# GLA gate function moved behind a PSUM copy, and softmax scaling moved to ScalarE, in a two-layer hybrid decoder kernel

## The chip, the cores and the metric

The kernel runs on one core of a Trainium2 chip, in one launch. The metric is the device time of that launch in microseconds (us). Below, PE is the matrix engine (PEld its weight loads), DVE the vector engine, ACT the scalar engine, POOL GpSimd, SP the engine that issues most DMAs. PSUM is the memory that PE writes, SBUF the working memory. All engines run their own instructions in a fixed order and wait for one another by semaphores.

## The reference

Two layers, 1024 tokens, width 1024, float32. A layer has a mixer and a channel part; the mixer runs gated linear attention (GLA, 4 heads) beside latent softmax attention (MLA, 4 heads) and projects both back. Cut to what the change touches:

```
# GLA: chunked linear attention with a data-dependent decay; then
o = gla_chunked(q, k, v, log_a)
o = rms_norm(o, gla_out_norm) * silu(g_o)            # g_o = columns of h @ w_in: the "gate"
# MLA: causal softmax attention, 128 queries at a time
s = (q_nope k_nope^T + q_pe k_pe^T) * scale
p = softmax(where(mask, s, -inf))
out = p v
mixed = concat([gla_out, mla_out]) ; x += gate_a * (mixed @ w_out)
# channel part
x += gate_f * (relu(h W1)^2 W2)
```

## The kernel before, in words

Every large product is made of three matmuls on rounded halves (`mm3`, lines 161 to 163: high times high, high times low, low times high). Weights arrive by DMA and are split into a high and a low part by ACT (line 314) and DVE (line 315). The channel part uses seven products instead of eight for a two by two block product; its lines are 1287 to 1290 (operands combined and split) and 1415 (results added).

The mixer works on two halves of the tokens, A and B, of 512 each. Its steps stand in a table of short words, `PROGRAM`: `L` latents, `T` what follows them, `Q` GLA queries and keys, `W` GLA scores, `v` and `g` GLA values and gates, `O` GLA outputs, `u`/`U` a head's queries and keys, `a` softmax attention of one head and two query blocks, and so on. `gA OA` stand next to each other, and so do `gB` and, after a few steps, `OB`.

GLA scores (`gla_scores`) walk through seven levels of a block hierarchy. A level has a decay update on DVE (lines 973, 978), exponentials on ACT (972, 974), products on POOL (944, 975), copies into block form on ACT (948), small matmuls into PSUM bank `g` (929) and masked writes from that bank on DVE (955, 983, 990). The bank has two buffers.

Gates (`gates`, lines 1029 to 1042) are four token blocks of 128 x 512 products in four PSUM banks. For each, ACT computes |x| from PSUM (1036), then exp and log (1037, 1038), DVE reads PSUM again for min(x,0) minus that (1039), ACT takes exp (1040), and DVE multiplies the PSUM product by it into SBUF (1041). The bank is free when 1041 is done.

In softmax attention (`softmax_pair`) DVE takes the row maximum (721), ACT the exponentials with their sum (736), DVE the reciprocal of the sum (740) and the scaling of the row block by it (741), before PE transposes the block (756), ACT and DVE split the transposed block (759, 760), and PE multiplies it with the values (lines 161 to 163 again).

The order on each engine is not the order of the code: a scheduler lists the instructions by what it takes to be ready, with the program's order as the priority. A change in one place moves instructions in many others.

Of the kernel before, what the change touches and what calls it, by code (L numbers as in the profile page):

```python
# [15 lines left out]
AF = mybir.ActivationFunctionType  # L16
ALU = mybir.AluOpType
# [109 lines left out]
def hybrid_kernel(  # L127
# [7 lines left out]
    V, S, G, PE = nc.vector, nc.scalar, nc.gpsimd, nc.tensor  # L135
# [16 lines left out]
    def bank_of(tags):  # L152
        i = turn.get(tags, 0)
        turn[tags] = i + 1
        return bank(tags[i % len(tags)])

    def tmp():
        return tp.tile([P, 512], F32, tag="t", name="tmp")

    def mm3(o, lh, ll, rh, rl, start, stop):  # L160
        PE.matmul(o, lh, rh, start=start, stop=False)  # L161
        PE.matmul(o, lh, rl, start=False, stop=False)  # L162
        PE.matmul(o, ll, rh, start=False, stop=stop)  # L163
# [251 lines left out]
    def bc(a, n):  # L415
        return a.unsqueeze(len(a.shape)).broadcast_to(list(a.shape) + [n])
# [195 lines left out]
    def inproj_tok(l, hf, kind, w, hs, tg):  # L612

        pss = [bank_of(tg) for _ in range(4)]
        for q in range(4):
            u = U[l, hf, kind, q]
            get(u)
            for t in range(4):
                for k2 in range(2):
                    h = hs[q * 2 + k2]  # L620
                    wh, wl = uw(u, k2, 0, w)
                    mm3(pss[t][:, 0:w], R(h[:, t * P:(t + 1) * P]), R(h[:, 512 + t * P:512 + (t + 1) * P]), wh, wl,
                        q == 0 and k2 == 0, q == 3 and k2 == 1)
            drop(u)
        return pss

    def layer_mixer(l, hA, make_hB):
# [70 lines left out]
        def softmax_pair(gp, Qn, Kn, Qr, ts_):  # L698
            Pt, pk = [], []
            for t in (2 * gp, 2 * gp + 1):  # L700
                n = (t + 1) * P
                hq, tq = t // 4, (t % 4) * P
                qh = R(Qn[hq][:, tq:tq + P])
                ql = R(Qn[hq][:, 512 + tq:512 + tq + P])
                qr = R(Qr[hq][:, tq:tq + P])
                nch = (n + 511) // 512
                nm = sp.tile([P, 2], F32, tag="nm", name="nm")
                sm = sp.tile([P, 2], F32, tag="sm", name="sm")
                pss = []
                for cc in range(nch):  # L710
                    w = min(512, n - cc * 512)
                    ps = bank_of(ts_)
                    o = ps[:, 0:w]
                    kh, kl = R(Kn[cc][:, 0:w]), R(Kn[cc][:, 512:512 + w])
                    mm3(o, qh, ql, kh, kl, True, False)
                    last = cc == nch - 1
                    PE.matmul(o, qr, R(kpe[cc][:, 0:w]), start=False, stop=False)
                    PE.matmul(o, qr, R(kpe[cc][:, 512:512 + w]), start=False, stop=not last)
                    if last:
                        PE.matmul(o[:, w - P:w], ident_bf, causal_bf, start=False, stop=True)  # L720
                    V.tensor_reduce(nm[:, cc:cc + 1], o, AX.X, ALU.max, negate=True)
                    pss.append((o, w))
                if nch == 2:
                    V.tensor_tensor(nm[:, 0:1], nm[:, 0:1], nm[:, 1:2], op=ALU.min)
                if gp == 1:
                    p_ = AR.alloc()
                    pk.append(p_)
                    p_ = p_[:, 0:n]
                elif gp == 0:
                    if t == 0: pk.append(AR.alloc())  # L730
                    p_ = pk[0][:, t * P:t * P + n]
                else:
                    p_ = AR.alloc()
                    pk.append(p_)
                for cc, (o, w) in enumerate(pss):
                    S.activation(p_[:, cc * 512:cc * 512 + w], o, AF.Exp, bias=nm[:, 0:1], accum_out=sm[:, cc:cc + 1])
                if nch == 2:
                    V.tensor_tensor(sm[:, 0:1], sm[:, 0:1], sm[:, 1:2], op=ALU.add)
                rc = sp.tile([P, 1], F32, tag="rc", name="rc")
                V.reciprocal(rc, sm[:, 0:1])  # L740
                V.tensor_scalar(p_[:, 0:n], p_[:, 0:n], rc, None, op0=ALU.mult)
                Pt.append(p_)
            return Pt, pk

# [74 lines left out]
        def used(hf):  # L819
            left[hf] -= 1  # L820
            if left[hf] == 0:
                AR.free(*hsb[hf])
# [206 lines left out]
        def gates(hf):  # L1029
            x = hv[hf]  # L1030
            x.g = [AR.alloc(), AR.alloc()]
            x.g3 = [a.rearrange("p (t n) -> p t n", t=2) for a in x.g]
            pss = inproj_tok(l, hf, "g", 512, hsb[hf], tags[5])
            for t in range(4):
                e = tmp()
                S.activation(e, pss[t], AF.Abs)
                S.activation(e, e, AF.Exp, scale=-1.0)
                S.activation(e, e, AF.Ln, bias=1.0)
                V.scalar_tensor_tensor(e, pss[t], 0.0, e, op0=ALU.min, op1=ALU.subtract)
                S.activation(e, e, AF.Exp)  # L1040
                V.tensor_tensor(x.g3[t // 2][:, t % 2, :], pss[t], e, op=ALU.mult)
            used(hf)

        def gla_out(hf):
            x = hv[hf]
            q, kdT, v3, g3, AT, eb = x.q, x.kdT, x.v3, x.g3, x.AT, x.eb
            ssq = sp.tile([P, 16], F32, tag="ssqg", name="ssqg")
            rst = sp.tile([P, 16], F32, tag="rstg", name="rstg")
            for tt in range(4):
                j, t = tt // 2, tt % 2  # L1050
                o = bank_of(tags[6])
                first = True
                if hf * 4 + tt > 0:
                    for p in range(2):
                        PE.matmul(o[:, p * 256:(p + 1) * 256], q[:, p * 512 + tt * P:p * 512 + (tt + 1) * P], state[:, p, :],
                                  start=first, stop=False, skip_group_check=True)
                        first = False
                for h in range(4):
                    PE.matmul(o[:, h * P:(h + 1) * P], AT[j][:, t * 512 + h * P:t * 512 + (h + 1) * P],
                              v3[j][:, t, h * P:(h + 1) * P], start=first, stop=(h == 3), skip_group_check=True)  # L1060
                    first = False
                if hf * 4 + tt < 7:
                    kvp = bank_of(tags[6])
                    for p in range(2):
                        PE.matmul(kvp[:, p * 256:(p + 1) * 256], kdT[:, (tt * 2 + p) * P:(tt * 2 + p + 1) * P],
                                  v3[j][:, t, p * 256:(p + 1) * 256], start=True, stop=True)
                    for p in range(2):
                        for e in range(2):
                            rs, cs_ = slice(e * 64, e * 64 + 64), slice(e * P, e * P + P)
                            st = state[rs, p, cs_]  # L1070
                            V.scalar_tensor_tensor(st, st, eb[rs, p * 4 + tt:p * 4 + tt + 1],
                                                   kvp[rs, p * 256 + e * P:p * 256 + (e + 1) * P], op0=ALU.mult, op1=ALU.add)
                sq = tmp()
                S.activation(sq, o, AF.Square)
                V.tensor_reduce(ssq[:, tt * 4:tt * 4 + 4], sq.rearrange("p (a n) -> p a n", a=4), AX.X, ALU.add)
                rstd_small(rst[:, tt * 4:tt * 4 + 4], ssq[:, tt * 4:tt * 4 + 4], ((0, 4, 128),), 4)
                gt = g3[j][:, t, :]
                g4 = gt.rearrange("p (a n) -> p a n", a=4)
                G.tensor_tensor(g4, g4, bc(rst[:, tt * 4:tt * 4 + 4], P), op=ALU.mult)
                V.tensor_tensor(gt, o, gt, op=ALU.mult)  # L1080
            x.mt = [AR.alloc(), AR.alloc()]
            for h in range(4):
                ps = bank_of(tags[6])
                for t in range(4):
                    PE.transpose(ps[:, t * P:(t + 1) * P], g3[t // 2][:, t % 2, h * P:(h + 1) * P], ident)
                S.activation(x.mt[h // 2][:, (h % 2) * 512:(h % 2) * 512 + 512], ps, AF.Identity, scale=gcol("go", l))
            AR.free(q, kdT, *x.v, *x.g, *AT)
# [368 lines left out]
```

## Time and profile before

| | |
|---|---|
| time, median of 3 runs | 2327.41 us (2325.14 to 2329.38) |
| profiled execution | 2325.83 us, span 2324.0 us |
| PE busy | 2226.7 us (96%) |
| DVE busy | 1777.6 us (76%) |
| ACT busy | 1135.3 us (49%) |
| POOL busy | 255.4 us (11%) |

The span is one execution as the hardware profiler saw it. A busy share is an average over very different stages, so the stage in which an engine waits matters more than its total. In the views below, "idle before" is the time for which an engine did nothing before an instruction, and the name behind the arrow is what ended that wait. Counts in a stretch that ends inside a step can split a pattern: 32 scalings per layer are 29 in the stretch that is used here.

### The profile page before, as it was taken

What the parts mean: (1) busy time and instruction counts of PE and PEld (TensorE: products, weight loads), DVE (VectorE), ACT (ScalarE), POOL (GpSimd) and SP (SyncE); (2) the same over time, 40 slices, a digit from 0 to 9 for tenths busy, and PEclk for the clock granted to TensorE, in tenths of its full rate; (3) what the DMA queues carried; (4) which work ended last, traced back from release to release, by engine and by line L of the source; (5) the groups of instructions that cost most, each with busy time, mean ns of one, the idle gap of its engine ahead of it and who ended that gap; (6) DMA issues with size and microseconds to landing.
All of it is one profiled execution on the core that took longest, in us unless ns stands there. A gap on an engine that the chain in (4) does not pass through costs nothing.

```text
span 2324.0 us, 29252 instructions
## 1 busy us (share of the span) xinstructions
PE 2226.7 (96%) x11016; PEld 1854.6 (80%) x11016; DVE 1777.6 (76%) x2519; ACT 1135.3 (49%) x1759; POOL 255.4 (11%) x236
## 2 busy tenths in 40 slices
PE   6979899999999998998999999999999999999998
PEld 3868788888788886887778888888888888877887
DVE  4887769757888888989894755997665867887794
ACT  3565646534732384433454545665365228633341
POOL 0042323100030000000011332320002000000000
PEclk8989999999999999999999999999999999999999
DMA  9632200136668655765784431004354654365462
GB/s 350 198 98 87 84 24 7 47 126 209 199 201 278 219 177 175 251 209 201 250 295 174 142 132 51 10 1 132 132 160 139 196 185 145 124 224 196 163 208 82
DMA packets 238450, 365.01 MB, mean 157 GB/s; under 512 B 11846, under 2 KB 146148, under 8 KB 238308
## 3 DMA queue, kind: packets, MB, share of 16 engines
q1 hardware_dynamic: 237760, 362.66, 47.5%
q8 instruction: 87, 1.43, 0.3%
q14 instruction: 55, 0.45, 0.1%
q10 hardware_dynamic: 548, 0.48, 0.1%
HBM read 325.73 MB, written 37.36 MB: 156 GB/s over the span
## 4 chain that ended last, share of the span: by engine, by line
PE 71%; DVE 11%; DMA 9%; issue 4%; ACT 2%; POOL 1%; SPq 0%; DVEq 0%; POOLq 0%; ACTq 0%
PE ps_m L162 9%; PE ps_m L163 9%; PE ps_m L161 9%; PE ps_s L162 7%; PE ps_s L163 7%; PE ps_s L161 7%; PE ps_g L163 4%; PE ps_g L162 4%; PE ps_g L161 4%; DMA s<-in_w_ada_dram 3%; DMA s<-in_w_mlp_down_dram 2%; PE ps_x L163 2%; PE ps_x L162 2%; PE ps_x L161 2%; DMA s<-in_w_mlp_up_dram 1%
## 5 line engine op out<-in xcount | busy, mean ns | idle before, releaser
L314 ACT CAST s<-s 128x1024 fp32r<-128x1024 f32 (+2 forms) x298 | 307.2, 1036 | 476.8 <-DVE s L311 259.2
L162 PE MATMUL ps_m<-s,s 128*128 128x512 f32 (+2 forms) x1212 | 460.9, 381 | 15.8 <-DVE s L1290 14.0
L161 PE MATMUL ps_m<-s,s 128*128 128x512 f32 (+2 forms) x1212 | 460.0, 383 | 10.6 <-ACT s L1289 4.7
L163 PE MATMUL ps_m<-s,s 128*128 128x512 f32 (+2 forms) x1212 | 457.0, 378 | 1.6 <-DVE s L315 1.6
L315 DVE TENSOR_TENSOR s<-s,s 128x1024 fp32r<-128x1024 f32 (+2 forms) x282 | 337.2, 1204 | 125.8 <-ACT s L314 105.5
L161 PE MATMUL ps_s<-s,s 128*128 128x512 f32 (+5 forms) x928 | 357.8, 389 | 5.0 <-ACT s L448 4.0
L163 PE MATMUL ps_s<-s,s 128*128 128x512 f32 (+5 forms) x928 | 355.5, 384 | 1.3 <-DVE s L315 1.3
L162 PE MATMUL ps_s<-s,s 128*128 128x512 f32 (+5 forms) x928 | 355.9, 384 | 0.0
L311 DVE TENSOR_TENSOR s<-s,s 128x1024 f32<-128x1024 f32 x160 | 198.9, 1245 | 117.2 <-DMA s<-in_w_mlp_up_dram 73.6
L162 PEld LDWEIGHTS ps_m<-s,s 128*128 128x128 f32 x1212 | 229.4, 189 | 60.9 <-DVE s L1290 17.4
L161 PEld LDWEIGHTS ps_m<-s,s 128*128 128x128 f32 x1212 | 229.1, 189 | 55.6 <-ACT s L1289 5.9
L163 PEld LDWEIGHTS ps_m<-s,s 128*128 128x128 f32 x1212 | 228.7, 189 | 41.9 <-DVE s L315 2.4
L1289 ACT CAST s<-s 128x1024 fp32r<-128x1024 f32 x140 | 146.8, 1051 | 185.5 <-DVE s L1287 53.3
L161 PEld LDWEIGHTS ps_s<-s,s 128*128 128x128 f32 x928 | 175.6, 189 | 40.6 <-ACT s L448 4.2
L163 PEld LDWEIGHTS ps_s<-s,s 128*128 128x128 f32 x928 | 175.8, 189 | 35.6 <-issue 1.9
L162 PEld LDWEIGHTS ps_s<-s,s 128*128 128x128 f32 x928 | 176.2, 190 | 32.0 <-issue 0.6
L162 PE MATMUL ps_g<-s,s 128*128 128x512 f32 (+1 forms) x506 | 195.2, 387 | 0.4 <-DVE s L1290 0.4
L161 PE MATMUL ps_g<-s,s 128*128 128x512 f32 (+1 forms) x506 | 194.6, 388 | 0.1
L163 PE MATMUL ps_g<-s,s 128*128 128x512 f32 (+1 forms) x506 | 194.4, 387 | 0.1
L1290 DVE TENSOR_TENSOR s<-s,s 128x1024 fp32r<-128x1024 f32 x140 | 171.2, 1227 | 13.3 <-ACT s L1289 9.7
L162 PE MATMUL ps_x<-s,s 128*128 128x512 f32 (+3 forms) x362 | 124.2, 345 | 1.9 <-DVE s L760 1.9
L161 PE MATMUL ps_x<-s,s 128*128 128x512 f32 (+3 forms) x362 | 122.4, 343 | 2.4 <-DVE s L760 2.4
(322 smaller groups left out, 3491.2 us busy)
## 6 DMA issues: line engine op xcount, KB each, us to landing
s<-in_w_mlp_up_dram SPq DMA_DIRECT2D x192, 512.0 KB
s<-in_w_mlp_down_dram SPq DMA_DIRECT2D x192, 512.0 KB
s<-in_w_ada_dram SPq DMA_DIRECT2D x80, 512.0 KB
s<-in_w_in_dram SPq DMA_DIRECT2D x36, 512.0 KB
s<-in_w_ada_dram SPq DMA_DIRECT2D x32, 256.0 KB
xd<-s SPq DMA_DIRECT2D x16, 512.0 KB
s<-in_w_out_dram SPq DMA_DIRECT2D x16, 512.0 KB
s<-xd SPq DMA_DIRECT2D x16, 512.0 KB
```

The lines of the kernel that those rows point to most:

```text
L161: PE.matmul(o, lh, rh, start=start, stop=False)
L162: PE.matmul(o, lh, rl, start=False, stop=False)
L163: PE.matmul(o, ll, rh, start=False, stop=stop)
L311: V.tensor_tensor(raw[:, :n], raw[:, :n], u.second[:, :n], op=ALU.add if u.sign > 0 else ALU.subtract)
L314: (V.tensor_copy if u.eng[-2] == "v" else S.copy)(R(u.hi[:, :n]), raw[:, :n])
L315: (V if u.eng[-1] == "v" else G).tensor_tensor(R(u.lo[:, :n]), raw[:, :n], u.hi[:, :n], op=ALU.subtract)
L1289: S.copy(R(hi), t)
L1290: V.tensor_tensor(R(lo), t, hi, op=ALU.subtract)
```

## The change

In `gates` each of the four PSUM products is now copied to SBUF by ACT and nothing else is done there. The gate function, unchanged in its arithmetic, stands at the head of `gla_out` and reads and overwrites the SBUF copy. In `softmax_pair` the scaling of the probabilities by the reciprocal of their sum is an ACT instruction with a per-partition scale instead of a DVE instruction. The lines behind the first change keep their text and shift by up to two; the gate function's lines 1036 to 1041 become 1045 to 1050, and the copy is line 1035.

```
-                V.tensor_scalar(p_[:, 0:n], p_[:, 0:n], rc, None, op0=ALU.mult)
+                S.activation(p_[:, 0:n], p_[:, 0:n], AF.Copy, scale=rc)
...
             for t in range(4):
-                e = tmp()
-                S.activation(e, pss[t], AF.Abs)
-                S.activation(e, e, AF.Exp, scale=-1.0)
-                S.activation(e, e, AF.Ln, bias=1.0)
-                V.scalar_tensor_tensor(e, pss[t], 0.0, e, op0=ALU.min, op1=ALU.subtract)
-                S.activation(e, e, AF.Exp)
-                V.tensor_tensor(x.g3[t // 2][:, t % 2, :], pss[t], e, op=ALU.mult)
+                S.copy(x.g3[t // 2][:, t % 2, :], pss[t])
...
         def gla_out(hf):
...
+            for tt in range(4):
+                gt, e = g3[tt // 2][:, tt % 2, :], tmp()
+                S.activation(e, gt, AF.Abs)
+                S.activation(e, e, AF.Exp, scale=-1.0)
+                S.activation(e, e, AF.Ln, bias=1.0)
+                V.scalar_tensor_tensor(e, gt, 0.0, e, op0=ALU.min, op1=ALU.subtract)
+                S.activation(e, e, AF.Exp)
+                V.tensor_tensor(gt, gt, e, op=ALU.mult)
             for tt in range(4):
```

DVE in the first layer's scores of half A, before; `s_165` and `s_166` hold the gates, `ps_m` and `ps_s` are their PSUM banks, `s_154` and `s_155` the scores:

```order
L990 COPY_PREDICATED s_154_1162<-lvm,ps_g 128x256x2
L973 TENSOR_TENSOR s_160_1171<-s_119_882 128x512
L1039 SCALAR_TENSOR_TENSOR tmp<-ps_m,tmp 128x512
L990 COPY_PREDICATED s_155_1163<-lvm,ps_g 128x256x2
L1039 SCALAR_TENSOR_TENSOR tmp<-ps_s,tmp 128x512
L1041 TENSOR_TENSOR s_165_1347<-ps_s,tmp 128x512
L978 TENSOR_TENSOR s_119_882<-s_119_882 128x32x16
L990 COPY_PREDICATED s_154_1162<-lvm,ps_g 128x128x4
```

And now, the stretch of the same engine in which the gate function's instructions stand:

```order
L990 COPY_PREDICATED s_154_1162<-lvm,ps_g 128x64x8
L1048 SCALAR_TENSOR_TENSOR tmp<-s_165_1347,tmp 128x512
L973 TENSOR_TENSOR s_161_1172<-s_119_882 128x512
L990 COPY_PREDICATED s_155_1163<-lvm,ps_g 128x64x8
L1048 SCALAR_TENSOR_TENSOR tmp<-s_165_1347,tmp 128x512
L1048 SCALAR_TENSOR_TENSOR tmp<-s_166_1348,tmp 128x512 x2
L978 TENSOR_TENSOR s_119_882<-s_119_882 128x16x32
L1050 TENSOR_TENSOR s_165_1347<-s_165_1347,tmp 128x512 x2
L990 COPY_PREDICATED s_154_1162<-lvm,ps_g 128x32x16
```

The eight DVE instructions of the gate function stay among the masked writes of the scores; they stand two levels later, and both their inputs are SBUF tiles.

ACT at the same place, now (before, the same instructions stand one by one between the others, each |x| read from a PSUM bank):

```order
L1035 COPY s_166_1348<-ps_m 128x512
L1035 COPY s_166_1348<-ps_s 128x512
L974 ACTIVATE s_160_1171<-s_160_1171 128x512
L1035 COPY s_165_1347<-ps_m 128x512
L1035 COPY s_165_1347<-ps_s 128x512
L972 ACTIVATE s_161_1172<-s_119_882 128x512
L1045 ACTIVATE tmp<-s_165_1347 128x512 x2
L1045 ACTIVATE tmp<-s_166_1348 128x512 x2
L314 CAST s_193_1741<-s_192_1739 128x1024
L948 COPY s_159_1167<-s_160_1171 64x8x64 x2
L974 ACTIVATE s_161_1172<-s_161_1172 128x512
L1046 ACTIVATE tmp<-tmp 128x512 x4
```

The gate function's ACT work comes in runs of four, ahead of copies (948) and exponentials (974) of the scores.

DVE in the first layer's attention, before, around the scaling of a block of 640 keys (`s_313` is the block):

```order
L738 TENSOR_TENSOR sm<-sm 128x1
L740 RECIPROCAL rc<-sm 128x1
L741 TENSOR_SCALAR s_313_3189<-s_313_3189,rc 128x640
L662 TENSOR_TENSOR s_308_3100<-ps_m,s_308_3100 128x256
L1075 TENSOR_REDUCE ssqg<-tmp 128x4
```

And ACT now, around the scaling of the same block:

```order
L736 ACTIVATE s_313_3197,sm<-ps_s,nm 128x512
L736 ACTIVATE s_313_3197,sm<-ps_s,nm 128x128
L646 COPY s_306_3078<-ps_m 128x384
L741 ACTIVATE s_313_3197<-s_313_3197,rc 128x640
L667 ACTIVATE s_309_3130<-s_306_3078 128x768
L1076 ACTIVATE tmp<-ps_g 128x512
L660 COPY s_307_3107<-ps_m 128x256
```

The scaling has left DVE's order and stands in ACT's, one copy behind the exponentials whose sum it needs, with a square (667) and PSUM copies (1076, 660) queued behind it.

## Rows read from the trace of the kernel before

**Rows 1.** Page, part 1: busy time of the engines, share of the span, instructions.
```profile
PE 2226.7 (96%) x11016; PEld 1854.6 (80%) x11016; DVE 1777.6 (76%) x2519; ACT 1135.3 (49%) x1759; POOL 255.4 (11%) x236
```
**Rows 2.** Windows: length, PE, PEld, DVE, ACT, POOL busy, PE clock, DMA share, GB/s.
```profile
143.00:183.00 40.00, 26.15 (x145) 24.01 (x145) 38.97 (x49) 29.05 (x48) 17.01 (x12) 0.79 0.18 51
260.00:290.00 30.00, 23.10 (x172) 20.82 (x171) 27.38 (x34) 25.34 (x45) 14.16 (x9) 1.00 0.26 74
320.00:475.00 155.00, 143.57 (x980) 127.64 (x978) 132.69 (x329) 93.85 (x244) 36.38 (x46) 0.97 0.12 36
...
1405.00:1430.00 25.00, 23.23 (x149) 21.19 (x148) 20.23 (x33) 17.66 (x35) 5.82 (x5) 0.93 0.17 56
1455.00:1580.00 125.00, 114.05 (x807) 101.48 (x806) 112.58 (x283) 82.67 (x216) 36.33 (x46) 0.99 0.05 14
```
**Rows 3.** PE's waits from 143 to 183 us, the longest: total, times, longest one.
```profile
PE ps_g L929 <- DVE s L990: 6.5, 6, 1.9
```
**Rows 4.** PE's waits from 260 to 290 us.
```profile
PE ps_g L929 <- DVE s L990: 2.9, 3, 1.2
PE ps_g L929 <- ACT s L948: 2.7, 2, 1.6
...
PE ps_s L161 <- DVE s L1041: 0.4, 1, 0.4
```
**Rows 5.** PE's waits from 320 to 475 us, the longest.
```profile
PE ps_x L756 <- DVE s L741: 1.9, 2, 1.3
PE ps_x L161 <- DVE s L760: 1.5, 2, 0.9
PE ps_g L756 <- DVE s L468: 1.5, 1, 1.5
PE ps_g L1065 <- DVE s L1080: 1.0, 1, 1.0
PE ps_m L161 <- ACT s L1093: 0.9, 1, 0.9
PE ps_x L162 <- DVE s L760: 0.9, 1, 0.9
PE ps_g L692 <- POOL s L607: 0.8, 1, 0.8
```
**Rows 6.** Timeline, DVE and PE near 356 us: start, length, what.
```profile
355.89 0.15 DVE L740 RECIPROCAL rc<-sm 128x1 f32<-128x1 f32 x1
...
356.69 1.15 DVE L741 TENSOR_SCALAR s<-s,rc 128x768 f32<-128x768 f32 x1
...
357.90 1.25 PE L756 MATMUL ps_x<-cs,s 128*128 128x128 f32 x6 [1.35 <-DVE s L741]
```
**Rows 7.** Line 741 on DVE from 320 to 475 us: count, busy us, mean ns.
```profile
L741 DVE TENSOR_SCALAR s<-s,rc 128x128 f32<-128x128 f32 (+7 forms) x29 | 14.9, 517 | 0.6
```
**Rows 8.** ACT instructions, run (L463, L1026) and 320 to 475 us: count, busy, mean.
```profile
L463 ACT ACTIVATE s<-tmp,mod 128x512 f32<-128x512 f32 x32 | 22.4, 730 | 13.1 <-DVE tmp L462 13.1
L1093 ACT CAST s<-s 128x512 fp32r<-128x512 f32 x8 | 5.0, 630 | 2.2 <-PE ps_m L163 2.1
L314 ACT CAST s<-s 128x1024 fp32r<-128x1024 f32 x3 | 3.1, 1049 | 4.8 <-DMA s<-in_w_out_dram 4.8
L1026 ACT COPY s<-ps_s 128x512 f32<-128x512 f32 x8 | 4.7, 587 | 13.8 <-PE ps_s L163 13.8
```
**Rows 9.** Lines 1039, 978, 424 on DVE: minimum, median, maximum ns, when.
```profile
L1039 DVE SCALAR_TENSOR_TENSOR tmp<-ps_m,tmp x8: 669/679/690, 146.3 to 1413.2; 128x512 f32<-128x512 f32 x8
L978 DVE TENSOR_TENSOR s<-s x28: 671/692/1814, 139.2 to 1404.4; 128x512 f32<-128x512 f32 x28
L424 DVE TENSOR_TENSOR s<-s,tmp x42: 676/685/693, 479.5 to 1695.6; 128x512 f32<-128x512 f32 x42
```
**Rows 10.** Timelines of DVE and POOL near 165 us.
```profile
164.69 1.56 POOL L944 TENSOR_TENSOR s<-s,s 128x512 f32<-128x512 f32 x1 [0.68 <-ACT s L972]
...
165.05 1.75 DVE L978 TENSOR_TENSOR s<-s 128x512 f32<-128x512 f32 x1
```

## The prediction

> **What bounds the kernel now.** I read the page's first part first: PE is busy for 2226.7 of 2324.0 us [rows 1]. DVE's 76% and ACT's 49% are averages, so neither is a bound by itself; what can be won lies in the 97 us in which PE does nothing, and the next question is where they are and who ends them. The windows answer the first half. The two stretches of GLA scores in the first layer leave PE idle for 13.9 us of 40 and 6.9 of 30, and there DVE is busy for 38.97 and 27.38 us: DVE is the bound. The two attention stretches leave it idle for 11.4 us of 155 and 10.9 of 125, with DVE at 86% and 90%. In the second layer the scores cost little, 1.8 of 25 us, because other matrix work stands between them [rows 2]. The waits give the second half: in the scores PE waits for the masked writes of line 990 (6.5 and 2.9 us), and in the second of them as long for ACT's copies, 2.7 us [rows 3, 4]; in attention nearly every wait is for DVE, the longest for the scaling that the change moves, 1.9 us [rows 5]. So both edits touch the engine that PE waits for.
>
> **The scaling goes to ACT.** It removes 29 instructions and 14.9 us from DVE in the first attention stretch [rows 7]. Their lengths grow with the keys, and ACT's I take from the nearest rows: 0.73 us for 512 columns with a per-partition operand, and (1049 - 630) / 512 = 0.82 ns for each further column [rows 8]. For 128 to 1024 columns that is 0.42 to 1.15 us, 6.3 us for one head's eight blocks, 0.79 on average, 22 to 23 us for the 29. Without the operand's 0.1 us it would be 19 to 20. DVE falls from 132.7 to 117.8 of 155 us, ACT rises from 93.9 to about 116.
>
> *What that frees.* One wait shows it: the reciprocal began at 355.89 and took 0.15, the scaling began only at 356.69 behind other DVE work and took 1.15, and PE lost 1.35 us [rows 6]. ACT's 0.94 us, begun behind the reciprocal, would end 0.8 us sooner. Of the 11.4 us idle, 0.9 are for ACT and twice 0.8 for POOL, so some 8 are for DVE [rows 5]. What waits behind a filled engine waits about as busy is to free: 86 to 14 before, 76 to 24 after, so by 46% less. That is 3.7 us a layer, 7.4 in both (the second stretch has the same pattern of waits and 10.9 us idle). The granted clock of the two stretches is 0.97 and 0.99, where PE had been waiting: 4.7 and 1.3 us worth of full clock [rows 2]. I let half go with the waits: 3.0. Together 10.4 us. The ends are nothing, if PE then waits for the next thing in DVE's order, and 22 us, if all these waits and the lost clock go.
>
> *What it adds.* A wait on ACT: the scaling stands behind a sum and a reciprocal on DVE, and ACT works in order, so the PSUM copies and squares behind it in ACT's list wait too, and PE for the banks. From below that is nothing, since the scheduler puts a copy or more between the exponentials and the scaling at many places. From above each of the 29 holds ACT for one DVE instruction, 132.69 / 329 = 0.40 us, 11.7 us a layer, all of it seen by PE. The nearest row is PE's present wait for ACT, 0.9 us; with ACT at 75% instead of 61%, busy to free doubles, so I add 0.9 a layer. The scaling itself is longer by 0.79 - 0.52 = 0.27 us at the two places where PE waited for it: 0.5 a layer. Together 2.8 us.
>
> **The gate function goes behind a copy.** The arithmetic stays; added are 16 ACT copies of 0.587 us, 9.4 us in all [rows 8]. The banks are free some microseconds earlier, but PE's only wait that the gates' last multiplication ends is 0.4 us [rows 4], so that is what this can give. The words "beside the outputs" do not hold in the built order: all eight DVE instructions of half A still stand among the masked writes, two levels later, and DVE's work up to the end of the scores is the same list. So the full DVE of that stretch isn't relieved.
>
> What differs is where they read. Reading one input from PSUM, line 1039 takes 0.669 to 0.690 us, every time. Two SBUF inputs take 0.685 where POOL is idle (line 424), but line 978 takes up to 1.814 [rows 9], and the long ones are those that met a POOL instruction: one began at 165.05 while POOL ran from 164.69 to 166.25, and ended at 166.80, a normal length after POOL's end [rows 10]. The Trainium skill (SBUF — State Buffer, Who interferes with whom) says that a VectorE instruction with two SBUF inputs, and GpSimd, take a shared port pair in turns, the loser blocked for the other's whole instruction, while one with at most one SBUF input does not contend; the trace agrees, and by that rule the change puts 32 more instructions under the lock, eight of them in each stretch where DVE is full. By rows: POOL is busy for 17.0 of 40 and 14.2 of 30 us, and meeting it costs half of its 1.56 us on average, so 8 x 0.43 x 0.78 = 2.7 and 8 x 0.47 x 0.78 = 2.9 us. I count half, 2.8, because the DVE instruction behind would often have waited for the same POOL instruction. The ends are 0.1 us (0.685 against 0.679) and 16 x 1.13 = 18 us, if each meets POOL at its start as line 978's longest did. In the second layer I count nothing: its scores are covered by the matrix work between them, and with that cover gone it would be the same 2.8. ACT's 2.4 us of copies per call are hidden in the first stretch by DVE, which ends later; in the second ACT goes from 25.3 to nearly 28 of 30, and if that shows it costs up to 2.4 us more.
>
> **The sum.** -10.4 + 2.8 + 2.8 - 0.4 = -5.2 us against the profiled execution's 2325.83, so 2320.6. The median of the runs shown is 1.6 us above that execution, which makes 2322 in the terms of the runs. A difference of 0.2%, 4.7 us, is what a measurement here can tell from no change, so the forecast sits just beyond it.
>
> **Rivals.**
> 1. *ACT takes DVE's place.* PE's waits of attention are only renamed, from line 741 on DVE to 741 on ACT and the copies behind it. For it: ACT is 61% busy there and goes to 75%, like DVE, and each scaling now crosses engines twice. Against it: one engine at 86% becomes two at about 76%. If ACT's waits come to 6 us a layer, half of the upper end, the sum is -10.4 + 12 + 2.4 = +4: 2331 us, just within 0.2%, and slower if they come to more.
> 2. *The port decides, and it is slower.* The place is the first layer's two scores stretches, the price that of rows 9 and 10 for instructions that meet POOL. It outweighs attention's net 7.6 us and the 0.4 at 0.5 us for each of 16 instructions, and makes the kernel slower by over 0.2% from about 0.8 us each. At 1.13 each it is +18 - 7.6 - 0.4: 2337 us. For it: DVE has next to nothing free there, and the runs of four on ACT push the exponentials that POOL needs later into the same stretch. Against it: POOL is idle for more than half of these stretches [rows 2]. The page of the Trainium skill named above (SBUF — State Buffer, Who interferes with whom) is the rule that speaks for this case.
> 3. *DVE's relief is worth all of it.* Both layers' waits for DVE (16 us) and the lost clock (6) go, less 5.2 of costs: -17, 2311 us. For it: single waits as that at 356 us go entirely. Against: lines 468, 760 and 1080 remain on DVE.
> 4. *The new order moves other waits.* The scheduler lists nearly the whole of both mixers anew, and the loads of the first layer's last products too. Of PE's 97 us idle, 97.3 - 44.9 = 52 stand outside the five stretches of rows 2, and neither edit speaks of them. I can't sign that; I let it widen every case by some 5 us, a tenth.
>
> **How the numbers follow.** The forecast gets 0.47, rival 1 0.25, rival 2 0.13, rival 3 0.15. Rival 4 spreads each by a few us: of the forecast 0.34 is faster, 0.12 the same and 0.01 slower; of rival 1 0.16 the same and 0.09 slower; of rival 3 0.14 faster and 0.01 the same; rival 2 is slower. Faster 0.48, same 0.29, slower 0.23. The range reaches from rival 3's 2311 to short of rival 2's full price: 2311 to 2334.
>
> **What would show it.** Right, if the two attention stretches are shorter by some 4 us each with DVE near 76% and ACT near 75%, PE's waits for lines 741 and 760 are half of what they were, and the first layer's scores take the same 38 us or one to three more with lines 1048 and 1050 at 0.9 us on average. The port is wrong if these are 0.69 throughout. Rival 1 is right if PE's waits name ACT lines 741, 660 and 759 with several us. The forecast is wrong if the attention stretches keep their length, or if the time is set by a stretch that has neither gates nor probabilities, above all the end of the first layer's channel part.

## The result, and the profile after

The changed kernel takes 2342.65 us, median of 4 runs (2336.95 to 2345.2), against 2328.2 for the kernel before beside it: ratio 1.0059, interval 1.0041 to 1.0077. It is slower by about 14 us, where 5 us faster were forecast and 2334 was the end of the range. A second measurement gave 1.0057 (1.0044 to 1.0070). Ratios here compare undisturbed executions on one chip, so they can differ a little from the quotient of two medians; a difference in us below is the ratio less 1, times 2328.

The page's first part, which answers [rows 1]: DVE has lost 14 us of work, ACT has gained 46, PE is busy 5.5 us longer with the same 11016 matmuls, and the span is 17.9 us longer, so PE does nothing for 12.4 us more.

```profile
span 2341.9 us, 29285 instructions
...
PE 2232.2 (95%) x11016; PEld 1857.4 (79%) x11016; DVE 1763.3 (75%) x2455; ACT 1181.7 (50%) x1839; POOL 251.0 (11%) x236
```

Since work moves between windows, I line the traces up by PE's work: each matmul counts with the median distance to its successor of its shape in the trace of before, and at equal sums the clocks of two traces are compared. The table gives, in us, by how much a stretch of before (named by its time there) is longer in another execution; "again" is a second execution of the same code, the others are the experiments below. PE's granted clock, as the windows below give it, is the mean over a stretch: 1.00 is the higher of its two levels throughout, 0.50 the lower.

| stretch of before | before, again | after, twice | scaling, twice | gates, both layers | gates, layer 0 | port alone | copies alone |
|---|---|---|---|---|---|---|---|
| 138 to 188, scores A, layer 0 | +0.3 | +1.2, +3.0 | -0.4, +0.2 | +2.1 | +3.0 | +2.5 | -1.4 |
| 266 to 301, scores B, layer 0 | -0.2 | +3.4, +6.2 | -0.1, 0.0 | +3.0 | +5.1 | +4.1 | +3.1 |
| 327 to 501, attention, layer 0 | -1.2 | -4.5, -4.5 | -4.3, -4.2 | +0.7 | +0.8 | +1.5 | +1.4 |
| 501 to 1068, channel part | +5.6 | +5.6, 0.0 | -0.6, +4.0 | +4.9 | +8.5 | +3.1 | +1.3 |
| 1068 to 1179, into layer 1 | -0.3 | +3.6, +3.9 | +0.9, +1.0 | +0.2 | -0.3 | +2.7 | +3.3 |
| 1179 to 1418, scores, layer 1 | -1.2 | -1.1, -0.9 | -0.9, -1.3 | -1.5 | -1.1 | +1.1 | +3.6 |
| 1418 to 1590, attention, layer 1 | -0.2 | +1.6, +2.5 | -3.4, -2.3 | +4.6 | -0.6 | +1.4 | +1.3 |
| 1590 to 1616, its end | +0.3 | +6.6, +4.5 | +5.1, +6.2 | +2.4 | +0.1 | 0.0 | 0.0 |

In the channel part the order on PE, DVE and ACT is the same in nearly all of them, and before itself came out 5.6 us apart: nothing is concluded from that row.

*Attention.* The windows that answer [rows 2]: stretch, length, then PE, PEld, DVE, ACT and POOL busy, clock, DMA share, GB/s.

```profile
143.00:186.00 43.00, 27.83 (x148) 25.46 (x148) 42.85 (x50) 33.71 (x55) 17.71 (x12) 0.80 0.17 47
268.00:301.00 33.00, 25.54 (x156) 22.53 (x155) 31.62 (x41) 22.64 (x42) 12.25 (x8) 0.90 0.12 36
325.00:478.00 153.00, 141.71 (x990) 124.95 (x989) 123.34 (x305) 112.22 (x278) 34.90 (x46) 1.00 0.13 40
...
1468.00:1595.00 127.00, 115.96 (x808) 102.21 (x807) 105.43 (x254) 95.22 (x236) 36.12 (x46) 0.99 0.05 14
1595.00:1640.00 45.00, 41.04 (x234) 35.54 (x233) 25.89 (x55) 25.81 (x53) 0.00 (x0) 0.92 0.43 129
```

In the first layer DVE is at 81% and ACT at 73% of a shorter stretch. But PE does nothing for 153 - 141.71 = 11.3 us in it, and did for 155 - 143.57 = 11.4 before: with DVE emptier, PE waits as long as it did. What got shorter is PE's own work, at a clock of 1.00 for 0.97: from 325.6 to 476.2 us it was busy for 139.3 us with the same 980 matmuls that took 143.6 before. A part of that is chance, since before's list ran at 0.98 and 0.99 in two other executions. In the second layer's stretch PE is idle for 127 - 115.96 = 11.0 us, and was for 10.9. PE's longest waits in the first layer, which answer [rows 5], no longer name line 741; in all they come to 9.1 us for DVE (8.2 before), 1.9 for ACT (0.9) and none for POOL (1.6):

```profile
PE ps_s L161 <- ACT s L736: 1.6, 2, 1.3
PE ps_g L692 <- DVE nm L724: 1.3, 1, 1.3
PE ps_x L756 <- DVE s L760: 1.2, 1, 1.2
```

The scalings themselves, which answer [rows 7], from 325 to 478 us (count, busy us, mean ns, idle time of ACT before them): 21.6 us, where 22 to 23 were expected; ACT stands idle 9.3 us in front of them until the reciprocal is there.

```profile
L741 ACT ACTIVATE s<-s,rc 128x128 f32<-128x128 f32 (+7 forms) x29 | 21.6, 760 | 9.6 <-DVE rc L740 9.3 <-ACT rs_y L409 0.3
```

At the end of the second layer's attention (1595 to 1640, clock 0.92) PE waits. Before, it was busy throughout, at 1.00 (first fence):

```profile
1582.00:1620.00 38.00, 37.99 (x229) 32.53 (x228) 26.63 (x61) 19.09 (x45) 0.00 (x0) 1.00 0.43 132
```
```profile
PE ps_x L161 <- ACT s L759: 2.4, 1, 2.4
PE ps_x L162 <- DVE s L760: 1.6, 1, 1.6
```

*Scores.* PE's waits from 138 to 190 us answer [rows 3]: 6.5 us for the masked writes have become 4.6, and two waits for ACT have come, the one for line 314 behind four instructions of the gate function in a row. As 2.8 us for line 983 and 0.9 for line 972 are gone, PE's waits for this bank sum to 10.0 us, and summed to 10.2 before.

```profile
PE ps_g L929 <- DVE s L990: 4.6, 3, 2.4
...
PE ps_g L929 <- ACT s L948: 2.9, 1, 2.9
PE ps_g L929 <- ACT s L314: 2.5, 1, 2.5
```

The gate function's two DVE lines (numbers are 9 higher now), to be held against line 1039 in [rows 9]: minimum, median and maximum in ns.

```profile
L1048 DVE SCALAR_TENSOR_TENSOR tmp<-s,tmp x16: 676/683/1752, 161.5 to 1429.2; 128x512 f32<-128x512 f32 x16
...
L1050 DVE TENSOR_TENSOR s<-s,tmp x16: 670/680/1756, 168.3 to 1431.6; 128x512 f32<-128x512 f32 x16
```

The median is as before; the maximum is that of an instruction which met POOL, as [rows 10] showed for line 978. The timelines of POOL and DVE show it on the new line: POOL runs two of line 944 from 160.34, line 1048 starts at 161.48 and takes 1.15, and the next one with two SBUF inputs meets the second for 1.74. On average the 16 of the first layer take 0.875 us.

```profile
160.34 3.40 POOL L944 TENSOR_TENSOR s<-s,s 128x512 f32<-128x512 f32 x2
```
```profile
161.48 1.15 DVE L1048 SCALAR_TENSOR_TENSOR tmp<-s,tmp 128x512 f32<-128x512 f32 x1
162.55 1.74 DVE L973 TENSOR_TENSOR s<-s 128x512 f32<-128x512 f32 x1
```

### The profile page after: what moved, and what is told of

Its sections match the earlier page's. It is cut to its first block, busy times and chain, and to the rows that moved or that the text cites. A ratio compares the mean times of both kernels' runs of the same rounds, so it can differ in the third digit from the quotient of the medians.

```text
span 2341.9 us, 29285 instructions
## 1 busy us (share of the span) xinstructions
PE 2232.2 (95%) x11016; PEld 1857.4 (79%) x11016; DVE 1763.3 (75%) x2455; ACT 1181.7 (50%) x1839; POOL 251.0 (11%) x236
```

## The experiments

**One half of the change each.** First: only the scaling goes to ACT.

```
-                V.tensor_scalar(p_[:, 0:n], p_[:, 0:n], rc, None, op0=ALU.mult)
+                S.activation(p_[:, 0:n], p_[:, 0:n], AF.Copy, scale=rc)
```

> The scaling alone goes to ACT; the gates stay as before. The built order on every engine is then that of the kernel before, except in the two attention stretches. Theory 1 (the gate function's move is what costs, the scaling gains): 2316 to 2324, that is 4 to 12 us faster than before, both attention stretches shorter. Theory 2 (the scaling costs, ACT in order being the new bound): 2335 to 2342, the loss lying in the second attention stretch and its end. Theory 3 (neither edit costs by itself; two further things do, the transfers of the first layer's channel part, which shift from execution to execution, and the end of the second attention): 2325 to 2333, the first attention some 5 us shorter, the end of the second some 6 us longer, the first layer's channel part longer by 0 to 7 us though its order is that of before.

Measured 0.9995 (0.9983 to 1.0007), and in a second measurement 0.9992 (0.9980 to 1.0004): no change that can be told. In the first attention PE does nothing for 152 - 141.71 = 10.3 us, 1.1 less than in before, with DVE at 81%; in the second (1449.7 to 1571.3 us) for 8.5, where it was 10.9. In the first its waits for DVE have fallen from 8.2 to 5.7 us, and those for ACT have risen from 0.9 to 4.3.

```profile
320.00:472.00 152.00, 141.71 (x983) 125.31 (x983) 123.88 (x304) 111.22 (x278) 35.37 (x46) 0.99 0.13 39
```

Second: only the gates.

```
-                e = tmp()
-                S.activation(e, pss[t], AF.Abs)
-                ...
-                V.tensor_tensor(x.g3[t // 2][:, t % 2, :], pss[t], e, op=ALU.mult)
+                S.copy(x.g3[t // 2][:, t % 2, :], pss[t])
 (and in gla_out the gate function on g3, as in the change)
```

> The gate function alone goes behind the copy; the scaling stays on DVE. Theory 1: 2335 to 2342, nearly all of the loss of both edits together. Theory 2: 2325 to 2331, since the scores of half A and B lost only 1 and 3 us with both edits. Theory 3: 2330 to 2338, 4 us of it in the first layer's scores, the rest in the first layer's channel part and the passage to the second layer, where the order is listed anew.

Measured 1.0059 (1.0043 to 1.0075), 13.7 us: the whole loss. Theory 1 is right on the gates and wrong that the scaling gains. Where the function is written doesn't matter: a kernel with the copy in place and the function left directly behind it, built but not run, has the very same lists on all five engines. The scheduler sets the order; what changed is what the function reads, and the copy. Both kernels were also run once more as they are.

> The changed kernel once more, for a second profile. Theories 1 and 2: 2338 to 2346, and the stretch from 500 to 1050 us, whose order is that of the kernel before, takes the same as in the first profile, 7 us longer than before. Theory 3: 2333 to 2346, and that stretch differs from the first profile by several us.

> The kernel before once more, for a second profile. All theories: 2325 to 2330. Theory 3 expects the stretch from 500 to 1050 us to differ from the first profile by up to 7 us; theories 1 and 2 by less than 1 us.

1.0057 (1.0044 to 1.0070), and 1.0003 (0.9993 to 1.0013) for before. The channel part went from +5.6 to 0.0 in the changed kernel with one list, so theory 3 has a varying stretch there, not a cause.

**By layers.** The gates in one layer only, and the scaling in the first layer only:

```
+                if l == 0:          (and l == 1 in the second kernel)
+                    S.copy(x.g3[t // 2][:, t % 2, :], pss[t])
+                else:
                 ... the function on the bank, as before
```
```
+                if l == 0:
+                    S.activation(p_[:, 0:n], p_[:, 0:n], AF.Copy, scale=rc)
+                else:
                     V.tensor_scalar(p_[:, 0:n], p_[:, 0:n], rc, None, op0=ALU.mult)
```

> The gate products are copied out of PSUM, and the gate function reads the copy, in the first layer only; the second layer's gates and all the scaling are as before. Theory 1 (the copies meet a full DVE and a nearly full ACT in the first layer's two scores stretches, and only there): the two stretches lose the 2 and 3 us that the run with both layers' gates lost there, the attention nothing, so 2333 to 2335 us, and the other layer's kernel nothing. Theory 2 (each layer pays by its new list, the second one in the attention that follows): about half of the 12 us here, 2333 to 2335 too, and as much in the other layer. Theory 3 (the loss of 5 us in the channel part of the first layer belongs to the change): 2337 to 2340 here and next to nothing in the other layer.

1.0037 (1.0023 to 1.0051), 8.6 us, with 3.0 and 5.1 us in the two scores stretches.

> As the kernel beside it, but in the second layer only. Theory 1: the second layer's scores are covered by matrix work, so 2327 to 2330 us. Theory 2: the 5 to 7 us that the run with both layers' gates lost between 1418 and 1616 us, so 2333 to 2336. Theory 3: 2327 to 2331.

0.9994 (0.9983 to 1.0005): nothing, as theory 1 said. The two don't add up to 13.7. The missing 6 us may be the 7 that the kernel with both layers' gates loses between 1418 and 1616, where its list differs from that of the kernel with the second layer's gates alone, though the source of the second layer is the same; no run separates that.

> The probabilities are scaled on ACT in the first layer only; all else as before. Theory 1 (the scaling gains some 4 us per attention stretch, and gives it back only at the end of the second layer's attention, where a weight cast that waits for its transfer stands in ACT's list ahead of a copy that PE needs): 2323 to 2325 us, faster than before by more than 0.1%. Theory 2 (no gain in the attention lasts, because transfers or the next stretch's waits set the end of the first layer): 2327 to 2330.

0.9973 (0.9962 to 0.9984): 6.3 us faster, so the first layer's gain lasts, and it is the second layer that gives it back.

**What in the scores costs.** In the first layer, the two causes apart: two SBUF inputs without a copy, and the copy without two SBUF inputs.

```
-                V.scalar_tensor_tensor(e, pss[t], 0.0, e, op0=ALU.min, op1=ALU.subtract)
+                src = e if l == 0 else pss[t]
+                V.scalar_tensor_tensor(e, src, 0.0, e, op0=ALU.min, op1=ALU.subtract)
 ...
-                V.tensor_tensor(x.g3[t // 2][:, t % 2, :], pss[t], e, op=ALU.mult)
+                V.tensor_tensor(x.g3[t // 2][:, t % 2, :], src, e, op=ALU.mult)
```

> The kernel before, but in the first layer the gate function's two DVE instructions read SBUF alone (the exponential's own tile in place of the bank with the product), with no copy out of PSUM. So the first layer's gate products are left out of the result. In the first scores stretch the lists of PE, DVE and ACT are those of the kernel before, so only the operands differ there. Theory 1 (two SBUF inputs against POOL are what the copies cost): the first scores stretch (138 to 188 us of before) is longer by 2 to 3 us and the second by 3, single gate instructions take up to 1.8 us, 2333 to 2337 us for 2328 before. Theory 2 (the four copies on ACT and the list that they bring, with runs of four of the same instruction, cost; the port little): the first stretch is as long as before within 1 us, 2327 to 2330.

```
+                if l == 0:
+                    S.copy(gt, pss[t])
-                S.activation(e, pss[t], AF.Abs)
+                S.activation(e, gt if l == 0 else pss[t], AF.Abs)
```

> The kernel before, with the copy of each gate product out of PSUM in the first layer, and the absolute value read from it; the two DVE instructions read the bank as before. So ACT's 16 x 0.57 us and the changed list are there, and two SBUF inputs are not. Theory 1 (the port): the scores stretches as before within 1 us each, 2327 to 2331. Theory 2 (ACT's copies and list): 2 to 3 us longer in the first stretch, 3 to 5 in the second, PE's waits there for ACT's lines 948 and 314 and not only for the masked writes: 2333 to 2337.

Port alone 1.0049 (1.0032 to 1.0065), copies alone 1.0045 (1.0030 to 1.0061), with eight more instructions on ACT and not the 16 of the expectation. The gate function's DVE lines in the first layer, of the one and of the other:

```profile
L1040 DVE SCALAR_TENSOR_TENSOR tmp<-tmp x8: 674/904/1779, 145.8 to 277.1; 128x512 f32<-128x512 f32 x8
...
L1042 DVE TENSOR_TENSOR s<-tmp x8: 669/676/1766, 150.4 to 280.5; 128x512 f32<-128x512 f32 x8
```
```profile
L1041 DVE SCALAR_TENSOR_TENSOR tmp<-ps_m,tmp x4: 666/674/693, 161.8 to 267.6; 128x512 f32<-128x512 f32 x4
L1041 DVE SCALAR_TENSOR_TENSOR tmp<-ps_s,tmp x4: 673/676/678, 164.7 to 281.1; 128x512 f32<-128x512 f32 x4
```

With a PSUM input none of the first layer's 16 takes over 0.71 us; with SBUF inputs alone, up to 1.78. In the first stretch this is the whole account. I sum there what the gate lines and lines 973 and 978 take over 0.69 us each, 21 instructions from 130 to 200 us: 6.4 us in before, 8.8 with the port alone, 5.1 with the copies alone, 8.8 with both. Busy us and mean ns of lines 973 and 978 in before, and of all four lines with the port alone:

```profile
L978 DVE TENSOR_TENSOR s<-s 128x512 f32<-128x512 f32 x7 | 8.0, 1145 | 0.0
L973 DVE TENSOR_TENSOR s<-s 128x512 f32<-128x512 f32 x6 | 7.3, 1215 | 0.0
```
```profile
L973 DVE TENSOR_TENSOR s<-s 128x512 f32<-128x512 f32 x6 | 7.2, 1204 | 0.0
L978 DVE TENSOR_TENSOR s<-s 128x512 f32<-128x512 f32 x7 | 7.0, 993 | 0.0
L1042 DVE TENSOR_TENSOR s<-tmp 128x512 f32<-128x512 f32 x4 | 4.6, 1160 | 0.0
L1040 DVE SCALAR_TENSOR_TENSOR tmp<-tmp 128x512 f32<-128x512 f32 x4 | 4.3, 1078 | 0.0
```

The differences, +2.3, -1.3 and +2.3, are what the table shows for the stretch: +2.5, -1.4 and +3.0. The changed kernel's two profiles fit too: +1.3 and +2.3 for +1.2 and +3.0. ACT's four copies and their order alone cost nothing there. In the second stretch the same sums, over 17 instructions, explain 2.4, 0.9 and 0.6 us of 4.1, 3.1 and 5.1. The rest, 1.7 to 4.5 us, belongs to ACT's copies, to the new list or to the granted clock (262 to 305 us: 1.00 in before, 0.96, 0.96 and 0.88 in these kernels), which no run separates.

Another part of their loss lies in the second layer, in source that is as before. Between 1307 and 1337 us of before the copies alone lose about 6 us and the port alone about 3.5. PE's wait there for a weight transfer, of before and then of the copies alone:

```profile
PE ps_m L162 <- DMA s<-wL: 0.8, 1, 0.8
```
```profile
PE ps_m L162 <- DMA s<-wL: 2.4, 1, 2.4
```

That is 1.6 us of it, and 1.0 with the port alone; waits for the scores' bank (line 929) give 1.3 more in both. Most of the rest is the granted clock: 0.91 over 36 us with the copies (from 1314) and 0.95 over 35 with the port (from 1315), 3.2 and 1.8 us worth, where it is 1.00 in before. So an edit of a few operands in one layer re-listed the next, and that list is the worse one. Theory 2 is refuted for the first stretch; the two totals, 11 us each, are above what either theory gave, for a reason that neither named.

**The function out of the scores.** In the changed kernel, the first instruction of each half's function is ordered behind the last copy of that half's scores.

```
+                first = S.activation(e, gt, AF.Abs)
+                tc.add_manual_dep(first.ins, x.end.ins.name, NOSYNC, reason="gates behind scores")
```

> The changed kernel, with the gate function's first instruction of each half ordered behind the last copy of that half's scores, so that no instruction of the gate function but the copy out of PSUM stands in the scores stretches. Theory 1 (the gate function's DVE and ACT work among the masked writes costs): the scores of the first layer are shorter by 4 to 9 us than in the changed kernel and shorter than before, and the 8 instructions of each half meet an engine that is less full in the attention: 2331 to 2337 us. Theory 2 (the second layer's attention pays for new lists): no better than the changed kernel by more than 3 us, 2340 to 2345, since the gate function now stands right at the start of the GLA outputs and PE waits for it or for the attention's DVE work behind it.

1.0048 (1.0030 to 1.0066), 11 us slower than before, which is theory 2's time but not by its cause. The scores are shorter than before, by 1.3 and 0.3 us, as theory 1 said, but about 9 us are lost between 241 and 266. The granted clock from 240 to 272 us is 0.89, where it was 1.00, 3.5 us worth, and PE waits there 5.6 us for a weight cast:

```profile
PE ps_s L161 <- ACT s L314: 5.6, 1, 5.6
```

and the cast 4.5 us for its transfer. In SP's order that transfer stands behind one that waits for a slot until line 870's transposes have read it: 12.4 us in before (first fence), 19.7 here (second), so the weights behind it leave later (244.75 for 236.02 us).

```profile
SPq L245 <- PE ps_x L870: 12.4, 1, 12.4
```
```profile
SPq L245 <- PE ps_x L870: 19.7, 1, 19.7
```

The work was moved out of one full stretch and came back as a late transfer.

**Why the second layer gives the scaling back.** The scaling on DVE for the second layer's last head, on ACT elsewhere:

```
+                if l == 0 or h < 3:      (ACT, else DVE as before)
```

> The probabilities are scaled on ACT in both layers, but for the second layer's last head, whose eight blocks are scaled on DVE as before; gates as before. Theory 1 (the end of the second layer's attention gives the gain back because the scaling makes ACT the late engine there): the end costs nothing, 2320 to 2323 us. Theory 2 (what costs there is where the scheduler puts the weight casts, and ahead of the last transposed block's copy one still stands): the 2.5 us wait behind the cast stays, 2323 to 2326.

0.9996 (0.9985 to 1.0008), with 6.8 us lost at the end and the wait still there (2.7 us): theory 1 falls, the last scalings themselves aren't the price. Theory 2's 2323 to 2326 us were missed as well. In ACT's list a weight cast stands ahead of a copy that PE needs. Two kernels, both with all the scaling on ACT, change that. One holds every later cast behind the last head's copies:

```
+        if u.eng[-2] != "v" and "copy" in ustate:
+            tc.add_manual_dep(c.ins, ustate["copy"], NOSYNC, reason="cast behind copies")
```

> All probabilities scaled on ACT in both layers, gates as before, and in the second layer each weight cast of ACT that is written after a copy of the last head's transposed probabilities is ordered behind it. Theory 1 (the scaling itself loads ACT too much at the end): the end of the attention (1590 to 1616 us of before) still loses 4 to 5 us, 2327 to 2330. Theory 2 (a cast that waits for its transfer holds up the copy behind it): PE's wait of 2.1 us for line 759 there goes and the end loses at most 2 us, 2322 to 2325, unless the casts, now four in a row behind the last copies, come too late for the output projection that reads them, which would show as PE waits for line 314 or 315 behind 1616 us.

0.9979 (0.9969 to 0.9990): the end loses nothing (-0.5) and the wait is gone, while the list that comes with it costs 1.7 us from 1560 to 1590, where the scaling alone gains 2.4. The other holds a single cast:

```
+        if u is U[1, "wo", 3]:
+            for name in ustate["copies"]:
+                tc.add_manual_dep(c.ins, name, NOSYNC, reason="cast behind copies")
```

> All probabilities scaled on ACT, gates as before, and one dependency added: in the second layer one weight cast of ACT (of the output projection's fourth unit) stays behind the last copy of transposed probabilities written before it. ACT's list differs from that of the kernel with the scaling alone by this one pair, swapped, and one pair further on. Theory 1 (ACT is too full at the end of the second layer's attention): nothing changes, 0.9975 to 1.000 of before. Theory 2 (the copy that PE needs stood behind a cast that waited for its transfer): PE's waits of 2.1 us for the copy and 1.6 for the subtraction behind it are gone or below 0.5 us, the step from 1590 to 1616 us falls from 5.1 to about 2, 0.996 to 0.9985 of before and 2 to 4 us less than the scaling alone.

> The scaling alone on ACT in both layers, once more, as the neighbour of the kernel with the swapped pair: 0.998 to 1.0005 of before by either theory, with PE's 2.1 us wait for the copy at the end of the second layer's attention.

0.9975 (0.9963 to 0.9986) with the pair swapped, 0.9992 (0.9980 to 1.0004) without, on the same chip. Beside ACT's pair the lists differ by little: DVE's subtraction behind the copy (760) stands one instruction earlier, three of PE's matmuls move, and one pair of the second channel part is swapped. ACT's timeline, without the swap and then with it, where lines stand 3 or 4 lower (start, length; in brackets the idle time before and what ended it):

```profile
1594.24 0.85 ACT L741 ACTIVATE s<-s,rc 128x640 f32<-128x640 f32 x1
1598.17 1.04 ACT L314 CAST s<-s 128x1024 fp32r<-128x1024 f32 x1 [3.08 <-DMA s<-in_w_out_dram]
1599.12 0.58 ACT L759 CAST s<-ps_x 128x512 fp32r<-128x512 f32 x1
```
```profile
1591.73 0.85 ACT L744 ACTIVATE s<-s,rc 128x640 f32<-128x640 f32 x1
1593.72 0.59 ACT L762 CAST s<-ps_x 128x512 fp32r<-128x512 f32 x1 [1.14 <-PE ps_x L759]
1596.15 1.05 ACT L314 CAST s<-s 128x1024 fp32r<-128x1024 f32 x1 [1.84 <-DMA s<-in_w_out_dram]
```

ACT stands 3.1 us in front of a cast whose weights are still under way, and the copy behind it, which PE waits for, starts 4.9 us after the scaling began; swapped, it starts 2.0 after. PE's waits at this end, without and with the swap:

```profile
PE ps_x L161 <- ACT s L759: 2.5, 1, 2.5
PE ps_x L162 <- DVE s L760: 1.5, 1, 1.5
```
```profile
PE ps_x L162 <- DVE s L764: 0.5, 1, 0.5
```

The end falls from +6.2 to +0.9 us: 4.0 of the 6.2 are these waits, and the granted clock, 0.89 there (1587.2 to 1619.5 us) and 1.00 with the swap, is worth most of the rest. In before the copy stood ahead of the cast:

```profile
1597.65 0.61 ACT L759 CAST s<-ps_x 128x512 fp32r<-128x512 f32 x1
1598.98 1.05 ACT L314 CAST s<-s 128x1024 fp32r<-128x1024 f32 x1 [0.73 <-DMA s<-in_w_out_dram]
```

Theory 2 is shown. The Trainium skill (PSUM — Partial Sum Buffer, Engine vs sequencer instructions) says that ScalarE's queue is strictly first in, first out; these rows agree: the copy came behind a cast in front of which ACT stood for 3.08 us. With 5.8 us gained, this kernel beats both before and after, as does the one with the first layer's scaling alone, at 6.3; the two intervals overlap.

## Why the prediction was wrong

**The scaling's term came near its total in one layer, and by another make-up.** It counted 7.6 us net for two layers, 3.8 each. Most of that was the step that PE's waits fall with DVE's busy share, "by 46%", 3.7 us a layer, and this step failed. DVE was relieved (to 81%, where 76% was forecast), and the instructions cost ACT what was expected. But PE's idle time went from 11.4 us to 11.3 in the first layer of the changed kernel and to 10.3 with the scaling alone, from 10.9 to 11.0 and to 8.5 in the second. With the scaling alone PE's waits for DVE did fall, by 2.5 us in the first layer, and those for ACT rose by 3.4, where 0.9 was counted; in the first layer of the changed kernel those for DVE rose too, to 9.1 us, as PE waited for other lines of it, which the prediction had as the lower end of its gain. The first layer alone gave 6.3 us (3.7 to 8.8) all the same: its attention came out 4.2 to 6.5 us shorter in the profiles of the kernels that change only the scaling, against 0 to 3.6 in executions of before's list, mostly by the granted clock (0.99 and 1.00, where before's list had 0.97 to 0.99), of which the prediction let only half go. That the totals meet is in part luck. In the second layer the attention gained 2.3 to 3.4 us up to 1590, and then lost 5 to 6, behind an engine order that I costed at nothing "from below" and 0.9 us as the value. My list of what ACT's wait holds up named PSUM copies and squares; it left out the weight casts, which wait for transfers. With them the question would have been where in the new list a cast comes ahead of a copy.

**The gate term was right on the port, and short by what it left at nothing.** Of 5.6 us for instructions under the port lock I counted half, 2.8, with the reason that the DVE instruction behind would often have met the same POOL instruction. The same sums for the two stretches put 2.3 and 0.6 us down to the port in the kernel with the first layer's gates, and 1.3 and 0.6 in the changed kernel (2.3 and 0.6 in its second profile): 1.9 to 2.9 us. The reason holds too: in the first stretch of the changed kernel the gate lines got 2.6 us longer and lines 973 and 978 1.3 shorter, with the port alone 3.5 and 1.1. What failed is the rest. For the first layer the sum had 2.8 - 0.4 = 2.4 us, and 8.6 (5.4 to 11.9) was measured. The copies in the second stretch, "up to 2.4 us more", were left at nothing, and that stretch lost 3.1 with the copies alone and 5.1 with the first layer's gates, 0.6 of them by the port. How the remainder divides among copies, order and clock stays open. The second layer's zero held for its scores.

**The rival without a sign had one.** "The new order moves other waits", some 5 us to either side, was much of the loss: between 1068 and 1179 the changed kernel loses 3.6 to 3.9 us in a list that neither half has alone (the port and copies kernels have it, and lose 2.7 and 3.3), and the gates of both layers lose 7 in the second attention. Of the unmeant moves told above, that at the end of the scaling, those of the port and copy kernels and that of the late gates were losses. Rival 2 gave 2337 us with the port at full price; the time came near it, but by the sums of lines 973, 978, 1048 and 1050 the port makes only 1.9 to 2.9 of the changed kernel's 14 us. Rival 3 is out. Rival 1 said what became of the waits: they were largely renamed. Its condition, 6 us for ACT in each layer, was not met in the first (1.9 us in the changed kernel, 4.3 with the scaling alone); in the second the changed kernel has 6.4 (1468 to 1640 us), 2.4 of them the wait for line 759 at the end.

**What was said to show it** came in part. Lines 1048 and 1050 took the 0.9 us on average that were forecast where the first layer's gates stand, and the first layer's attention was 4.5 us shorter. But the second layer's was 1.6 and 2.5 us longer in the two profiles, which was a sign of being wrong, and PE's waits for line 760 in the first were 2.1 us for 2.4, not half. The scores were longer by 4.6 and 9.2 us in the two profiles, where nothing to three were allowed.

## What to carry to other kernels

An operand moved from PSUM to SBUF is not free on DVE while POOL works: price it by the rows of instructions that meet POOL, less what the DVE instructions around them then no longer lose; here that was 1.3 to 2.3 us in the one stretch where DVE is full. An emptier engine does not by itself shorten the waits of the engine that bounds the kernel: before a busy share is turned into a gain, look up what that engine would wait for next, on the engine that takes the work too, and its granted clock. When work moves to an engine that also has instructions waiting for transfers, look in its new list for one of those ahead of an instruction that the bound engine waits for; here one swapped pair was worth about 4 us. With a scheduler, an edit of arithmetic is an edit of order everywhere behind it, so try each half and each layer alone before a sum is believed.

## What the runs showed that I had not expected

The same kernel's 570 us of channel part, with one order, differed by 5.6 us between two profiled executions, more than the effect that was forecast; a single profile can't place a few microseconds there. PE's granted clock differs likewise: 0.97, 0.98 and 0.99 in the first attention, in three executions of one list. And the DVE time lost to POOL in the first scores stretch answered PE's delay to within 0.7 us in all four kernels; DVE has nothing free there (42.85 of 43 us in the changed kernel).
